# Expert rows gathered in fp32 from the residual rows, one-hot columns that carry the norm factor, separate sums, and weight tiles up to 19 ahead

## The chip, the cores and the metric

The kernel runs on one core of a Trainium2 chip. The metric is the device time of one execution in microseconds (us). TensorE (PE in the profile) multiplies; VectorE (DVE), ScalarE (ACT) and GpSimd (POOL) work elementwise; every DMA is issued from SyncE's queue (SP), in program order.

## The reference

One transformer block over 512 tokens of width 1024, in fp32: a mixer (differential attention and a state-space branch, merged and projected into the residual) and then a mixture of experts. The second part is what the change touches:

```python
x = x + merged @ w_out[l]
h2 = rms_norm(x, norm_ffn_w[l], NORM_EPS)          # x * rsqrt(mean(x*x)+eps) * w
# hierarchical_moe(h2): 64 experts, each token goes to the best 2 of its best group of 8
xb = t[buf_tok].reshape(n_blocks, MOE_BLOCK, d)    # rows of h2, gathered by expert
hid = jax.nn.silu(xblk @ w_gate[e]) * (xblk @ w_up[e])   # 1024 -> 512
yb = hid @ w_down[e]                                      # 512 -> 1024
out = zeros.at[buf_tok].add(yb * buf_w[:, None])
return rms_norm(x + out, final_norm_w, NORM_EPS)
```

All 64 experts' weights are read once: 64 x 6 MB.

## The kernel before

The 512 tokens are four chunks of 128 rows. Up to the output projection the program is ordered by a small planner (`Flow`): each piece of work is a job with an engine, a cost, a priority and the jobs that it waits for, and the jobs are written into the program in the order in which the planner would start them. The last units, `WO0` and `WO1`, are the output projection; their handler `ev_wo` adds the result to the residual rows `x1`, sums squares, transposes the rows, computes the router's logits, and makes the norm factor of each row, `fst[:, 3]`.

*The normed rows.* `ev_wo` also makes h2: VectorE multiplies the residual by the norm's weight (`b`, L1291), ScalarE multiplies by the row's factor and rounds to fp32r (`hh`, the high part `h2H`), and VectorE or GpSimd subtracts to get the low part `h2L` (`hl` L1353, `hd` L1348). These are four big buffers.

*The router.* `route` works on chunks 0 and 1, then on 2 and 3, almost wholly on VectorE: the best group, the two best experts, then the place of each token within its expert (`rank` on TensorE, `rk`). `onehot` (L1434) writes a one-hot matrix `P` for the experts of the next two groups: 128 tokens by 256 slots for each chunk.

*The gather.* `gather_mm` (L1445, L1446) gathers the rows of a 128-column block `k` for 256 slots with eight fp32r matmuls (high and low part of each chunk), and ScalarE copies the result to `xt`.

*The experts.* 19 groups: the first 12 experts in pairs (64 slots each), the others in fours (32 slots each). The order of groups is two pairs, six fours, four pairs, seven fours. For a group, `gate_up` (L1714) multiplies 8 blocks `k` against the gate and up weights, 2 or 4 experts side by side in TensorE's columns; then come the activation, `hidden_t` (transposes), `down` (L1737) and `weighted`. The results go back to the tokens with `combine` (L1753, L1754, and the add to `x1`, L1759), which runs one group later, right after the next group's `gate_up`. After an odd group's `combine` and `hidden_t`, and ahead of its `down`, stands the gather for the next two groups. For the first two groups the gather is spread over group 0's `gate_up` (one block ahead of each `k`).

*The weights.* An expert's weights come as six tiles of 1 MB, each for two blocks `k`: four for gate/up, two for down. `tiles` lists them in the order of use. `issue` sends the next one into a big buffer, into the extra buffer `ewx` or into the pair of staging buffers; `free` and `fill` are called after every second `k`: as many tiles as were used up are counted free, and as many are issued. There are 19 big buffers (`NB`). Two hold `x1`, four `h2H` and `h2L`; so 13 big ones, `ewx` and the staging pair hold weights: 15 tiles. `NS = 4` experts are first in order whatever the counts; the others are placed by counts that group 0 works out (`perm`).

Of the kernel before, what the change touches and what calls it, by code (L numbers as in the profile page):

```python
# [118 lines left out]
def block_kernel(ctx: ExitStack, tc: tile.TileContext, I, out):  # L119
# [1092 lines left out]
    NX = 2  # L1212
    NE = NB - 6 + NX
# [11 lines left out]

    def issue():
        n = nxt["i"]
        nxt["i"] += 1
        kind, e, q = tiles[n]
        if n % NE == XS:  # L1230
            t = [stage(), stage()]
        else:
            b = (mt("ewx", [128, 2048], "ew") if n % NE == 0 else big("ew")).rearrange("p (k n) -> p k n", k=2)
# [5 lines left out]
        if n % NE == XS:  # L1239
# [6 lines left out]
    x1t, h2H, h2L = [], [], []  # L1246
# [4 lines left out]
    def consts():  # L1251
        m = mt("xt", [128, 2048], "rc")
        rc["nfw"] = m[:, :1024]
        nc.sync.dma_start(rc["nfw"], bcast(I["nfw"], D))
        rc["wr"] = m[:, 1024:1600].rearrange("p (k n) -> p k n", k=8)
        nc.sync.dma_start(rc["wr"], I["wr"])
        nft = m[:, 1600:1608]
        nc.sync.dma_start(nft, I["nft"])
        V.tensor_tensor(rc["wr"], rc["wr"], nft.unsqueeze(2).to_broadcast([128, 8, 72]), op=OP.mult)
        rc["lgh"] = m[:, 1608:1896].rearrange("p (c n) -> p c n", c=NCH)  # L1260
        rc["br"] = m[:, 1896:1968]
# [8 lines left out]

    cj = J("Q", 2.5, consts, [fpj, wsl], prio=-1)
# [3 lines left out]
    lgj, lmj, hlj, h2j = {}, {}, {}, {}  # L1275

    def ev_wo(n):
        def f(c, ps, j):
# [7 lines left out]

            def b(i):
                if i == 0:
                    t["hc"] = mt("y" if c else "P", [128, D], "hc")
                o = slice(i * 512, i * 512 + 512)  # L1290
                V.tensor_tensor(t["hc"][:, o], x1(c)[:, o], rc["nfw"][:, o], op=OP.mult)  # L1291
# [50 lines left out]
            def hs():  # L1342
                A.activation(t["hc"], t["hc"], AF.Copy, scale=fst[:, 3, c:c + 1])

            def hd():
                if c % 2 == 0:
                    h2L.append(big("h2L", F32R).rearrange("p (c n) -> p c n", c=2))
                G.tensor_tensor(h2L[c // 2][:, c % 2], t["hc"], h2H[c // 2][:, c % 2].bitcast(F32), op=OP.subtract)  # L1348

            def hl():  # L1350
                if c % 2 == 0:
                    h2L.append(big("h2L", F32R).rearrange("p (c n) -> p c n", c=2))
                V.scalar_tensor_tensor(h2L[c // 2][:, c % 2], t["hc"], fst[:, 3, c:c + 1],  # L1353
                                       h2H[c // 2][:, c % 2].bitcast(F32), op0=OP.mult, op1=OP.subtract)

# [8 lines left out]
            if n == 0:  # L1364
                t["a0"] = a_
            else:
                b_ = J("V", 0.61, lambda: b(0), [t["a0"], cj, hlj[1] if c == 3 else None, j if c < 3 else None],
                       prio=0.7 if c < 2 else 0.12)
                b_ = J("V", 0.61, lambda: b(1), [a_, b_], prio=0.7 if c < 2 else 0.12)
# [14 lines left out]
            else:  # L1384
# [5 lines left out]
                big_ = ["big"] if c % 2 == 0 else []  # L1390
                h_ = J("A", 1.0, hh, [s, b_, h2j.get(c - 1)], prio=2, acq=big_)
                h2j[c] = h_
                pl = hlj.get(c - 1) if c % 2 else None
                if c > 1:
                    h_ = J("A", 1.0, hs, [h_], prio=1)
                    hlj[c] = J("G", 2.35, hd, [h_, pl], prio=0, acq=big_)
                else:
                    hlj[c] = J("V", 1.2, hl, [h_, pl], prio=2, acq=big_)
# [29 lines left out]
    def onehot(es, cs=range(NCH)):  # L1428
        n, w = len(es), E if es[0] < NW else E // 2
        if 0 in cs:  # L1430
            R["P", es[0]] = mt("P", [128, NCH, 256], "P", F32R)
# [7 lines left out]
    def h2(t, c):  # L1439
        return t[c // 2][:, c % 2]  # L1440
# [9 lines left out]
    def route(cl, prev):  # L1450
# [51 lines left out]
        def gat(k):  # L1502
            if cl[0] == 0:
                gb[k] = side()
            gather_mm(R["P0"], 256, gb[k][:, :256], k, cl)
# [17 lines left out]
        kj = J("V", 0.2 + 0.35 * n, rk, [rj, r.get("rk", hlj[0])], prio=pr)  # L1523
        r["rk"] = kj
        last = cl[-1] == NCH - 1
        for k0 in (0, 1):
            j = J("P", 0.22 * n, lambda k0=k0: gat(k0), [kj, lmj[3]] + [hlj[c] for c in cl] + [r.get(("g", k0))],
# [13 lines left out]
    def evac(k):  # L1541
        if k == 0:
            xt[0] = mt("xt", [128, 8, 256], "xt")
        A.activation(xt[0][:, k], gb[k][:, :256], AF.Copy)
# [4 lines left out]
    def weights1():  # L1549
        V.tensor_copy(R["cnt"], R["rps"][:, 256:256 + E])  # L1550
        V.tensor_reduce(R["gs"], R["ge"], axis=AX.X, op=OP.add)
        V.reciprocal(R["gate"], R["gs"])
# [20 lines left out]
    live = {"n": NB - len(fl.tok["big"]) + 1}  # L1573

    def free(n=1):
        live["n"] -= n

    def fill():
        while nxt["i"] < len(tiles) and live["n"] < NB + NX:
            live["n"] += 1  # L1580
            issue()
# [93 lines left out]
    def gather1(P, xt, k):  # L1675
        ps = side()
        gather_mm(P, 256, ps[:, :256], k, range(NCH))
        A.activation(xt[:, k], ps[:, :256], AF.Copy)

    def gather(P, w, xt, ks=range(8), ps={}):  # L1680
        for k in ks:
            if k % 2 == 0:
                ps[0] = side()
            gather_mm(P, w, ps[0][:, (k % 2) * w:(k % 2) * w + w], k, range(NCH))
            if k % 2:
                A.activation(xt[:, k - 1:k + 1], ps[0][:, :2 * w].rearrange("p (k n) -> p k n", k=2), AF.Copy)
# [4 lines left out]
    def slots(P, n, w, wcols):  # L1691
        W = n * w
        ps = side()
        for c in range(NCH):
            T.transpose(ps[:W, c * 128:c * 128 + 128], P[:, c].bitcast(F32), ident)
        pt = mt("pt", [128, 512], "pt", F32R)[:W]
        V.tensor_copy(pt, ps[:W])
        ws = side()
        for c in range(NCH):
            T.matmul(ws[:W, :n], lhsT=P[:, c].bitcast(F32), rhs=wcols(c), start=(c == 0), stop=(c == 3))  # L1700
# [5 lines left out]
    def gate_up(xt, n, w, gu, done, pre=lambda q: None):  # L1706
# [24 lines left out]
    def down(ht, n, w, dn, done):  # L1731
# [25 lines left out]
    def combine_add(ps, c, i):  # L1757
        o = x1(c)[:, i * 512:i * 512 + 512]
        V.tensor_tensor(o, o, ps, op=OP.add)  # L1759

    def combine(pt, yh, yl):
        for c in range(NCH):
            for i in range(2):
                combine_add(combine_mm(pt, yh, yl, c, i), c, i)

    def odd(k):
        free(k % 2)
# [8 lines left out]
    ordering = order_tables()  # L1776
    for gi, g_ in enumerate(groups):
# [210 lines left out]
```

## Time and profile before

| | |
|---|---|
| median of 3 runs | 1835.35 us (1835.19 to 1837.14) |
| profiled execution: its own time | 1836.18 us |
| its span, first to last instruction | 1834.4 us |
| TensorE busy | 1621.0 us (88%) |
| VectorE, ScalarE, GpSimd busy | 786.0, 414.9, 321.4 us |
| read from HBM | 471.56 MB |
| granted TensorE clock, mean | 0.95 |

Up to about 850 us the mixer and its projection run. The expert weights are 403 MB of the 471 MB. A busy TensorE is not one at its peak: matmuls that wait one behind the other for weights count as busy too.

### The profile page before, as it was taken

What the parts mean: (1) busy time and instruction counts of PE and PEld (TensorE: products, weight loads), DVE (VectorE), ACT (ScalarE), POOL (GpSimd) and SP (SyncE); (2) the same over time, 40 slices, a digit from 0 to 9 for tenths busy, and PEclk for the clock granted to TensorE, in tenths of its full rate; (3) what the DMA queues carried; (4) which work ended last, traced back from release to release, by engine and by line L of the source; (5) the groups of instructions that cost most, each with busy time, mean ns of one, the idle gap of its engine ahead of it and who ended that gap; (6) DMA issues with size and microseconds to landing.
All of it is one profiled execution on the core that took longest, in us unless ns stands there. A gap on an engine that the chain in (4) does not pass through costs nothing. (4 is left out here: it accounts for less than half of the span.)

```text
span 1834.4 us, 22989 instructions
## 1 busy us (share of the span) xinstructions
PE 1621.0 (88%) x8767; PEld 995.2 (54%) x8767; DVE 786.0 (43%) x1487; ACT 414.9 (23%) x839; POOL 321.4 (18%) x331
## 2 busy tenths in 40 slices
PE   8999999999999999998996877778998777787785
PEld 6878788878787777887451423124444231132232
DVE  7698842487878765436130521021321211111113
ACT  5355530344444432122110100001011000010001
POOL 5244421153526252102000000000000000000001
PEclk8999999999999999999999889889999898898988
DMA  5321123222121222356899999999999999999995
GB/s 160 102 62 49 53 85 99 70 69 81 59 92 58 69 70 92 92 214 275 335 388 420 419 421 421 420 420 420 421 419 420 421 419 421 421 419 420 421 420 225
DMA packets 81616, 475.19 MB, mean 259 GB/s; under 512 B 10208, under 2 KB 10592, under 8 KB 35808
## 3 DMA queue, kind: packets, MB, share of 16 engines
q1 hardware_dynamic: 81504, 473.70, 65.5%
q8 instruction: 70, 1.15, 0.3%
q14 instruction: 42, 0.34, 0.1%
HBM read 471.56 MB, written 2.10 MB: 258 GB/s over the span
## 5 line engine op out<-in xcount | busy, mean ns | idle before, releaser
L1714 PE MATMUL g<-ew,xt 128*32 128x512 f32 (+1 forms) x1896 | 412.9, 691 | 151.8 <-DMA ew<-in_gu_dram 151.5
L243 PE MATMUL g<-hH,w 128*128 128x512 f32 x1024 | 345.6, 401 | 0.0
L1714 PEld LDWEIGHTS g<-ew,xt 128*32 128x32 f32 (+1 forms) x1896 | 96.2, 128 | 437.9 <-DMA ew<-in_gu_dram 273.8
L1719 DVE SCALAR_TENSOR_TENSOR hh<-hh,g 128x512 f32<-128x512 f32 x19 | 13.1, 687 | 504.9 <-ACT hh L1718 504.9
L243 PEld LDWEIGHTS g<-hH,w 128*128 128x128 f32 x1024 | 192.4, 188 | 43.7 <-issue 6.0
L243 PE MATMUL g<-hL,w 128*128 128x512 f32 x512 | 199.9, 390 | 0.0
L1737 PE MATMUL s<-ew,hT 128*32 128x512 f32 (+1 forms) x968 | 172.3, 653 | 23.0 <-DMA ew<-in_dn_dram 22.1
L1889 POOL TENSOR_TENSOR fst<-fst 128x1 f32<-128x1 f32 x4 | 1.2, 300 | 960.8 <-ACT fo L1882 960.7
L203 DVE TENSOR_TENSOR w<-stg,w 128x1024 fp32r<-128x1024 f32 x108 | 140.8, 1312 | 55.4 <-ACT w L200 32.2
L1718 ACT ACTIVATE hh<-g 128x512 f32<-128x512 f32 x19 | 11.3, 597 | 524.6 <-PE g L1714 524.6
L1737 PEld LDWEIGHTS s<-ew,hT 128*32 128x32 f32 (+1 forms) x968 | 46.3, 122 | 129.9 <-issue 77.7
L198 POOL TENSOR_SCALAR w<-stg 128x1024 fp32r<-128x1024 f32 x60 | 69.7, 1162 | 256.5 <-DMA stg<-in_wu_dram 178.8
L243 PEld LDWEIGHTS g<-hL,w 128*128 128x128 f32 x512 | 96.4, 188 | 16.8
L1759 DVE TENSOR_TENSOR x<-x,s 128x512 f32<-128x512 f32 x152 | 92.4, 678 | 23.0 <-PE s L1754 23.0
L1747 DVE SCALAR_TENSOR_TENSOR yl<-s,sl,yh 128x512 fp32r<-128x512 f32 x38 | 28.4, 751 | 163.8 <-ACT yh L1746 162.6
L848 DVE SCALAR_TENSOR_TENSOR xb<-u,cw,xb 128x511 f32<-128x511 f32 (+2 forms) x96 | 81.7, 861 | 23.4 <-ACT xb L844 21.7
L243 PE MATMUL g<-w,hH 128*128 128x512 f32 x256 | 84.5, 411 | 0.0
L1714 PE MATMUL g<-stg,xt 128*32 128x512 f32 (+1 forms) x152 | 81.6, 673 | 1.7 <-DMA stg<-in_gu_dram 1.6
L243 PE MATMUL g<-sH,w 128*128 128x512 f32 x256 | 80.7, 397 | 0.0
L200 ACT ACTIVATE w<-stg 128x1024 fp32r<-128x1024 f32 x60 | 63.2, 1054 | 76.8 <-DMA stg<-in_wu_dram 63.2
L1445 PE MATMUL s<-P,h2H 128*128 128x256 f32 (+1 forms) x320 | 78.5, 287 | 1.4 <-DVE P L1434 1.4
L1446 PE MATMUL s<-P,h2L 128*128 128x256 f32 (+1 forms) x320 | 76.7, 282 | 0.0
(338 smaller groups left out, 2454.2 us busy)
## 6 DMA issues: line engine op xcount, KB each, us to landing
ew<-in_gu_dram SPq DMA_DIRECT2D x237, 1024.0 KB, 18.3
ew<-in_dn_dram SPq DMA_DIRECT2D x118, 1024.0 KB, 18.5
stg<-in_wu_dram SPq DMA_DIRECT2D x120, 512.0 KB, 3.6
stg<-in_gu_dram SPq DMA_DIRECT2D x38, 512.0 KB, 17.7
stg<-in_dn_dram SPq DMA_DIRECT2D x13, 512.0 KB, 18.0
xT<-in_xT_dram SPq DMA_DIRECT2D x4, 512.0 KB, 5.7
x<-in_xn_dram SPq DMA_DIRECT2D x2, 1024.0 KB, 10.0
out_dram<-fo SPq DMA_DIRECT2D x8, 256.0 KB, 2.1
```

The source lines that it names most:

```text
L198: G.tensor_scalar(c["h"], c["st"], 1.0, 0.0, op0=OP.mult, op1=OP.add)
L200: A.activation(c["h"], c["st"], AF.Copy)
L203: (G if i % 10 == 9 else V).tensor_tensor(c["lo"], c["st"], c["h"].bitcast(F32), op=OP.subtract)
L243: T.matmul(cell[b], lhsT=x, rhs=y, start=first and i == 0, stop=last and i == 2)
L848: V.scalar_tensor_tensor(x()[:, 3 - k:], t["u"][:, :n], w[:, k:k + 1], x()[:, 3 - k:], op0=OP.mult, op1=OP.add)
L1445: T.matmul(o, lhsT=h2(h2H, c)[:, d], rhs=P[:, c], start=(c == 0), stop=False)
L1446: T.matmul(o, lhsT=h2(h2L, c)[:, d], rhs=P[:, c], start=False, stop=(c == NCH - 1))
L1714: T.matmul(o[es_], lhsT=xt[:, k, es_], rhs=gu(e, k)[:, i * 512:i * 512 + 512], start=(k == 0), stop=(k == 7), tile_position=(0, w * e))
L1719: V.scalar_tensor_tensor(hh, hh, 1.0, pg[:W], op0=OP.add, op1=OP.mult)
L1737: T.matmul(ps[i][es_], lhsT=ht[:, k, es_], rhs=dn(e, k)[:, i * 512:i * 512 + 512], start=(k == 0), stop=(k == 3), tile_position=(0, w * e))
L1747: V.scalar_tensor_tensor(yl[:, i], ps[i][:W], sl[:, :1], yh[:, i].bitcast(F32), op0=OP.mult, op1=OP.subtract)
L1759: V.tensor_tensor(o, o, ps, op=OP.add)
```

## The change

The split copies go. The gather multiplies the residual rows `x1` themselves, in fp32, one matmul for each chunk; the one-hot entry is the row's norm factor in place of 1, and the norm's weight is the scale of ScalarE's copy to `xt`. `x1` must therefore stay as it is, and the sums go to two buffers of their own, `acct`: the first `combine` reads `x1` and writes `acct`, the later ones add there. The token weights are divided by the norm factor again (the product with `fst[:, 3]` in `weights1`), and the one-hot for the way back is made by a comparison with 0.

Group 0's interleaved gather fetches only its own 128 slots; those of group 1 are gathered on their own, two blocks ahead of group 0's `down` and six in group 1's `gate_up`. The one-hot for groups 2 and 3 moves from group 0 to the end of group 1's `gate_up`. `issue` takes any free place (`room`): 17 big buffers, `ewx` and the staging pair, 19 tiles; when group 1 begins, two big ones are set aside for `acct`.

```diff
+    homes = []
+    room = {"ewx": 1, "stg": 0, "big": 0}
...
+            home = next(r for r in ("ewx", "stg", "big") if room[r] > (1 if r == "stg" and n < XS else 0))
+        room[home] -= 1
+        homes.append(home)
...
-            def hh():
-                if c % 2 == 0:
-                    h2H.append(big("h2H", F32R).rearrange("p (c n) -> p c n", c=2))
-                A.activation(h2H[c // 2][:, c % 2], t["hc"], AF.Copy, scale=fst[:, 3, c:c + 1])
...
-                G.tensor_tensor(h2L[c // 2][:, c % 2], t["hc"], h2H[c // 2][:, c % 2].bitcast(F32), op=OP.subtract)
...
         for c in cs:
-            V.tensor_tensor(P[:, c].rearrange("p (e s) -> p e s", e=n),
-                            rk1[:, c, es[0]:es[0] + n].unsqueeze(2).to_broadcast([128, n, w]),
-                            iota1[:, None, :w].to_broadcast([128, n, w]), op=OP.is_equal)
+            if es[0] == 0:
+                for e in range(n):
+                    V.tensor_scalar(P[:, c, e * w:e * w + w], iota1[:, :w], rk1[:, c, e:e + 1], fst[:, 3, c:c + 1],
+                                    op0=OP.is_equal, op1=OP.mult)
...
+        if es[0]:
+            scaled(P)
...
-    def gather_mm(P, w, o, k, cs):
+    def scaled(P):
+        V.tensor_tensor(P, P, fst[:, 3].unsqueeze(2).to_broadcast([128, NCH, P.shape[2]]), op=OP.mult)
+
+    def gather_mm(P, o, k, cs):
         d = slice(k * 128, k * 128 + 128)
         for c in cs:
-            T.matmul(o, lhsT=h2(h2H, c)[:, d], rhs=P[:, c], start=(c == 0), stop=False)
-            T.matmul(o, lhsT=h2(h2L, c)[:, d], rhs=P[:, c], start=False, stop=(c == NCH - 1))
+            T.matmul(o, lhsT=x1(c)[:, d], rhs=P[:, c], start=(c == 0), stop=(c == NCH - 1))
+
+    def gathered(xt, k, ps):
+        A.activation(xt[:, k], ps, AF.Copy, scale=rc["nft"][:, k:k + 1])
...
-    live = {"n": NB - len(fl.tok["big"]) + 1}
+    room.update(stg=1, big=len(fl.tok["big"]))
...
         def pre(k):
-            if gi == 0:
-                if 1 <= k < 7:
-                    gather1(P, xt, k + 1)
-                if k in ordering:
-                    ordering[k]()
+            if gi < 2 and 1 <= k < 7:
+                half = slice(128 * gi, 128 * gi + 128)
+                gather(P[:, :, half], xt[:, :, half], [k + 1])
+            if gi == 0 and k in ordering:
+                ordering[k]()
+            if gi == 1 and k == 7:
+                nP[0] = onehot(sum(groups[2:4], []))
...
+        if gi == 1:
+            room["big"] -= 2
...
-            if gi + 2 < NG:
-                es = sum(groups[gi + 2:gi + 4], [])
-                P = onehot(es)
+            if gi == 0:
+                gather(P[:, :, 128:], xt[:, :, 128:], [0, 1])
+            elif gi + 2 < NG:
+                nP[0] = onehot(sum(groups[gi + 2:gi + 4], []))
         elif not last:
-            m = P.shape[2]
-            xt = rows(m)
-            gather(P, m, xt)
+            P = nP[0]
+            xt = rows(P.shape[2])
+            gather(P, xt)
             ps_ = group_slots(P, gi + 1)
```

TensorE between group 0's transposes and group 1's gate/up, before (a row is one matmul, x16 sixteen of them; `hh` and `hT` are the hidden rows, `ident` the identity for transposes):

```order
L1726 MATMUL s<-ident,hh 128x128 x4
L1695 MATMUL s<-ident,P 128x128 x4
L1700 MATMUL s<-ptab,P 128x2 x4
L1737 MATMUL s<-ew,hT 64x512 x16
L1714 MATMUL g<-ew,xt 64x512 x32
```

and now, in the changed program:

```order
L1700 MATMUL s<-ident,hh 128x128 x4
L1669 MATMUL s<-ident,P 128x128 x4
L1674 MATMUL s<-ptab,P 128x2 x4
L1422 MATMUL s<-P,x_6945 128x128 x2
L1422 MATMUL s<-P,x_7000 128x128 x2
L1422 MATMUL s<-P,x_6945 128x128 x2
L1422 MATMUL s<-P,x_7000 128x128 x2
L1711 MATMUL s<-ew,hT 64x512 x16
L1688 MATMUL g<-ew,xt 64x512 x4
L1422 MATMUL s<-P,x_6945 128x128 x2
L1422 MATMUL s<-P,x_7000 128x128 x2
L1688 MATMUL g<-ew,xt 64x512 x4
```

Gather matmuls (L1422) now stand ahead of group 0's down stage, and four of them between the gate/up matmuls of two blocks; this goes on for six blocks of group 1.

VectorE in the router, from the second half's logits of chunk 2 to the first one-hot matrices, before (`x_7000` are the residual rows of chunks 2 and 3, `ht` transposed rows, `lg` logits, `ab` the chosen experts, `ptab` the places):

```order
L1285 SCALAR_TENSOR_TENSOR x_7000<-g,x_7000 128x256 x2
L1327 SCALAR_TENSOR_TENSOR lg<-s,fst,rc 128x72
L1291 TENSOR_TENSOR hc<-x_7000,rc 128x512
L1309 COPY ht<-s 128x256
L1331 TENSOR_TENSOR fst<-fst 128x1
L1332 TENSOR_SCALAR fst<-fst 128x1
L1309 COPY ht<-s 128x256
L1479 TENSOR_TENSOR d_6972<-o_6973,o_6974 128x16
L1480 TENSOR_TENSOR ab<-og,d_6972 128x128
```

and now:

```order
L1459 TENSOR_TENSOR ab<-og,d_6972 128x128
L1295 SCALAR_TENSOR_TENSOR x_7000<-g,x_7000 128x256 x2
L1477 SCALAR_TENSOR_TENSOR ptab<-s,ab 128x128
L1406 TENSOR_SCALAR P<-iota_93,ptab,fst 128x64 x8
L1313 COPY ht<-s 128x256
L1335 TENSOR_TENSOR fst<-fst 128x1
L1336 TENSOR_SCALAR fst<-fst 128x1
L1331 SCALAR_TENSOR_TENSOR lg<-s,fst,rc 128x72
L1313 COPY ht<-s 128x256
```

The router's first half (`ab` of chunks 0 and 1) now stands ahead of the last residual add instead of behind the copies of the transposed rows, and the eight one-hot instructions of chunks 0 and 1 stand ahead of those copies.

## Rows read from the trace of the kernel before

**Rows 1.** Windows: stretch, its length, engines' busy us (instructions), clock, DMA share, GB/s.

```profile
865.00:870.00 5.00, 5.00 (x24) 3.40 (x24) 3.18 (x18) 0.86 (x3) 0.00 (x0) 0.71 0.00 0
...
880.00:890.00 10.00, 10.00 (x59) 5.25 (x60) 0.34 (x2) 1.75 (x5) 0.00 (x0) 1.00 0.82 313
...
930.00:935.00 5.00, 5.00 (x26) 1.72 (x24) 0.00 (x0) 0.00 (x0) 0.00 (x0) 1.00 0.37 107
935.00:940.00 5.00, 5.00 (x43) 1.34 (x42) 1.50 (x2) 1.37 (x2) 0.00 (x0) 1.00 1.01 416
...
1300.00:1400.00 100.00, 98.23 (x522) 50.32 (x520) 29.11 (x56) 12.49 (x20) 0.00 (x0) 1.00 1.02 420
```

**Rows 2.** Waits: SyncE's queue in 860 to 936 us; TensorE in 936 to 1815 us.

```profile
SPq L1243 <- PE s L1737: 23.3, 3, 16.0
...
PE g L1714 <- DMA ew<-in_gu_dram: 151.5, 109, 2.7
```

**Rows 3.** Timeline of SyncE's queue, 915 to 940 us: start, length, engine, instruction.

```profile
915.83 17.38 SPq L1243 DMA_DIRECT2D ew<-in_gu_dram  x3
```

**Rows 4.** Timeline of TensorE's matmuls in groups 0 and 1.

```profile
867.90 1.94 PE L1714 MATMUL g<-ew,xt 128*64 128x512 f32 x8
869.77 0.39 PE L1445 MATMUL s<-P,h2H 128*128 128x256 f32 x1
...
870.91 1.94 PE L1714 MATMUL g<-ew,xt 128*64 128x512 f32 x8
...
901.91 13.90 PE L1714 MATMUL g<-ew,xt 128*64 128x512 f32 x64
915.74 0.50 PE L1753 MATMUL s<-yh,pt 128*128 128x512 f32 x1
...
919.61 0.66 PE L1726 MATMUL s<-ident,hh 128*128 128x128 f32 x4
920.21 0.38 PE L1445 MATMUL s<-P,h2H 128*128 128x256 f32 x1
...
927.88 0.60 PE L1695 MATMUL s<-ident,P 128*128 128x128 f32 x4
...
929.20 0.64 PE L1737 MATMUL s<-ew,hT 128*64 128x512 f32 x1
```

**Rows 5.** Timeline of TensorE: other fp32 matmuls of 128 columns.

```profile
853.53 1.25 PE L303 MATMUL s<-ident 128*128 128x128 f32 x8
...
888.80 1.16 PE L1633 MATMUL s<-ox,tT 128*128 128x128 f32 x8
889.89 0.64 PE L1714 MATMUL g<-stg,xt 128*64 128x512 f32 x1
```

**Rows 6.** Timeline of the router's stretch: TensorE, GpSimd and VectorE.

```profile
847.07 3.02 PE L243 MATMUL g<-w,gt 128*128 128x512 f32 x12
849.13 2.36 POOL L1348 TENSOR_TENSOR h2L<-hc,h2H 128x1024 fp32r<-128x1024 f32 x1 [3.07 <-ACT hc L1343]
849.19 2.33 DVE L1475 SCALAR_TENSOR_TENSOR es<-o,es 128x16 f32<-128x16 f32 x1
...
852.46 0.75 DVE L1285 SCALAR_TENSOR_TENSOR x<-g,x 128x256 f32<-128x256 f32 x2
853.32 0.68 DVE L1291 TENSOR_TENSOR hc<-x,rc 128x512 f32<-128x512 f32 x1
...
857.65 2.34 POOL L1348 TENSOR_TENSOR h2L<-hc,h2H 128x1024 fp32r<-128x1024 f32 x1 [2.44 <-ACT hc L1343]
857.99 2.63 DVE L1434 TENSOR_TENSOR P<-ptab,iota 128x256 fp32r<-128x256 f32 x2
...
862.30 0.18 DVE L1475 SCALAR_TENSOR_TENSOR es<-o,es 128x16 f32<-128x16 f32 x1
...
864.87 0.76 DVE L1434 TENSOR_TENSOR P<-ptab,iota 128x256 fp32r<-128x256 f32 x2
...
871.47 0.53 DVE L1613 TENSOR_SCALAR ox<-iota,ox 64x64 f32<-64x64 f32 x2
```

More of the change, by code (lines that the diff above doesn't have):

```diff
@@ L1269, in x1, with res @@
         return x1t[c // 2][:, c % 2]
+    def res(c):
+        return acct[c // 2][:, c % 2]
     cj = J("Q", 2.5, consts, [fpj, wsl], prio=-1)
@@ L1572, in block_kernel @@
     fl.run()
-    live = {"n": NB - len(fl.tok["big"]) + 1}
+    room.update(stg=1, big=len(fl.tok["big"]))
     def free(n=1):
-        live["n"] -= n
+        for _ in range(n):
+            room[homes.pop(0)] += 1
     def fill():
-        while nxt["i"] < len(tiles) and live["n"] < NB + NX:
-            live["n"] += 1
+        while nxt["i"] < len(tiles) and max(room.values()) > 0:
             issue()
@@ L1672, in overflow_tables, with gather @@
         V.tensor_copy(R["ovi"], ef)
[L1675 to L1680, printed above, removed]
-        for k in ks:
[L1682 to L1686, printed above, removed]
+    def gather(P, xt, ks=range(8)):
+        w = P.shape[2]
+        for k in ks:
+            ps = side()[:, :w]
+            gather_mm(P, ps, k, range(NCH))
+            gathered(xt, k, ps)
     def rows(w):
@@ L1694, in slots @@
         for c in range(NCH):
-            T.transpose(ps[:W, c * 128:c * 128 + 128], P[:, c].bitcast(F32), ident)
+            T.transpose(ps[:W, c * 128:c * 128 + 128], P[:, c], ident)
         pt = mt("pt", [128, 512], "pt", F32R)[:W]
-        V.tensor_copy(pt, ps[:W])
+        V.tensor_scalar(pt, ps[:W], 0.0, None, op0=OP.is_gt)
         ws = side()
         for c in range(NCH):
-            T.matmul(ws[:W, :n], lhsT=P[:, c].bitcast(F32), rhs=wcols(c), start=(c == 0), stop=(c == 3))
+            T.matmul(ws[:W, :n], lhsT=P[:, c], rhs=wcols(c), start=(c == 0), stop=(c == 3))
         sl = pools["mp"].tile([128, 1], F32, name="sl", bufs=2)[:W]
@@ L1729, in hidden_t, with down @@
         return ht
-    def down(ht, n, w, dn, done):
+    def down(ht, n, w, dn, done=lambda k: None):
         ps = [side(), side()]
@@ L1755, in combine_mm, with combine_add, combine @@
         return ps
[L1757 to L1761, printed above, removed]
+    def combine_add(ps, c, i, src=res):
+        h = slice(i * 512, i * 512 + 512)
+        V.tensor_tensor(res(c)[:, h], src(c)[:, h], ps, op=OP.add)
+    def combine(pt, yh, yl, src=res):
         for c in range(NCH):
+            if src is x1 and c % 2 == 0:
+                acct.append(big("acc").rearrange("p (c n) -> p c n", c=2))
             for i in range(2):
-                combine_add(combine_mm(pt, yh, yl, c, i), c, i)
-    def odd(k):
-        free(k % 2)
+                combine_add(combine_mm(pt, yh, yl, c, i), c, i, src)
     def group_slots(P, gi):
@@ L1807, in block_kernel @@
         elif not last:
-            combine(*pend)
+            combine(*pend, src=x1 if gi == 1 else res)
         if last:
@@ L1862, in block_kernel @@
         yo = [yo[:, 0], yo[:, 1]]
-        combine(pt1, *weighted(down(ht, 1, E, lambda e, k: ow["dn", k], odd), E, sl1, yo))
+        combine(pt1, *weighted(down(ht, 1, E, lambda e, k: ow["dn", k]), E, sl1, yo))
     fl.t = {e: 0.0 for e in "PVAGQ"}
@@ L1881, in sqr @@
             def sqr(i=i, c=c, o=o, half=half):
-                A.activation(o[:, half], x1(c)[:, half], AF.Square, accum_out=fst[:, i, c:c + 1])
+                A.activation(o[:, half], res(c)[:, half], AF.Square, accum_out=fst[:, i, c:c + 1])
             j = J("P", 0.43, mm, prio=c, acq=["s"])
@@ L1899, in f1 @@
         def f1(c=c, o=o):
-            A.activation(o[:, 512:], x1(c)[:, 512:], AF.Copy, scale=fst[:, 3, c:c + 1])
+            A.activation(o[:, 512:], res(c)[:, 512:], AF.Copy, scale=fst[:, 3, c:c + 1])
         def f2(c=c, o=o):
```

89 lines of the change are left out of this document (31 added, 58 removed).

## The prediction

> **What bounds the kernel now.** I read the windows first. From about 935 us to the end the weight stream runs at 416 to 420 GB/s without a dip, even in 1300 to 1400 us where TensorE is busy for 98.23 of 100 us; before 935 us it does dip: 0 GB/s at 865 to 870 us, 313 GB/s at 880 to 890 us, 107 GB/s at 930 to 935 us [rows 1]. Then the waits: after 936 us TensorE's large wait is for expert weights (151.5 us in 109 waits), while before 936 us the DMA queue waits for TensorE, once for 16.0 us at a down matmul [rows 2]. So there are two regimes. In the first two expert groups TensorE is the bound and the stream stops for want of buffers; from 935 us on the stream is the bound, and TensorE's idle time pays for what is added to it. The end of the kernel is therefore the moment at which the stream starts for the last time, plus the bytes still to come, plus a tail that the change leaves alone.
>
> That moment can be seen. The queue issues two tiles at 915.83 us and the third of that row only at the row's end, about 932.9 us [rows 3]. Counted in the code, it is tile 35 (from 0): 15 buffers for weights (13 of 19 big ones, the extra one, the staging pair), and 20 tiles given back by then: eight gate/up and four down tiles of group 0, eight gate/up tiles of group 1. Tile 35 needs the first down tiles of group 1, and that down stage starts at 929.20 us, after combine, transposes and the whole gather for groups 2 and 3 [rows 4].
>
> **The change part by part.** After it, two accumulators take the place of the four split copies, so 17 buffers hold weights once group 1 has begun (19 before). By the same count, the tile that waits for the first down tiles of group 1 is number 37. A tile is 1024 KB, at 420 GB/s 2.50 us, so two more tiles sent before the stop are worth -5.0 us. That is all that the extra buffers give: however early the first 19 tiles land, the stream has run dry again before that down stage. What TensorE does between the last work of the router and that down stage then counts in full.
>
> (a) *fp32 gather matmuls of 128 columns.* The trace of before has no gather in fp32, so its price comes from other fp32 matmuls; each stands there as two records. Four with different weights and 128 columns take 888.80 to 889.89 us: 0.136 us a record; the warm-keeping ones take 1.25/8 = 0.156 [rows 5]. Half of the 512-column price below would be 0.217, a quarter 0.109: that is the lower bound, 0.156 the upper, and I take 0.137, the row of the same shape. Group 0's six interleaved gathers cost 8 x 0.137 = 1.10 us each, against 1.14 us now (869.77 to 870.91) [rows 4]: nothing. New on the path are the second half's gathers: two before group 0's down, 16 records, +2.2 us (1.7 to 2.5), and six inside group 1's gate/up, 48 records, +6.6 us (5.2 to 7.5).
>
> (b) *The gather for groups 2 and 3.* Now 64 matmuls, 920.21 to 927.88 us = 7.67 us. Then 32 fp32 matmuls, 64 records of 256 columns. Price: 64 records of 512 columns, two experts side by side, take 13.90 us [rows 4], so one alone would be 2 x 0.217 = 0.434, and 256 columns 0.217; the combine matmuls (one pass, 512 columns, new weights each) take (919.61 - 915.74)/16 = 0.242. Twice the 128-column price would be 0.274, the upper bound. I take 0.23: 14.7 us, +7.0 us (+6.2 to +9.9).
>
> By a rule of the Trainium skill ("FP8 and Floating Point Precision", TensorE Precision Notes) a true fp32 product takes four passes. At 2.4 GHz that makes 0.213 us a matmul at 128 columns and 0.427 at 256, an estimate of 6.8 us for (a) and +6.0 us for (b). The 512-column row fits it (0.869 against 0.853 us), the 128-column row is above it (0.272 against 0.213). By the Trainium skill alone the sum below would be +5.3 us; I go by the rows.
>
> (c) *The start of group 0.* VectorE carries this stretch. TensorE's last output-projection matmul ends near 850.1 us, yet its result is read at 852.46, because VectorE sits in one 128x16 instruction for 2.33 us; the same line takes 0.18 us later. It lies beside a GpSimd subtraction for a split copy (849.13 us), which goes: -2.2 us. The multiply at 853.32 us goes: -0.6. The first one-hot pair took 2.63 us beside another such subtraction and becomes eight 64-column instructions; two of that kind take 0.53 us, so 2.1 us: -0.5. The second pair was undisturbed at 0.76 us and becomes 2.1: +1.3 [rows 6]. That makes -2.0. In the new order the first eight stand ahead of the copy of the last transposed rows and hold up the router's last logits, while the router's first half, no longer delayed, can end before the projection does; I put half a us on the second and take -2.5. Bounds: -4.0 (the eight at 0.18 us each make it -3.3, and the first half is won in full besides) and -1.0 (the logits lose half of the first item).
>
> (d) *At no cost:* the scaling of later one-hot matrices and their new place in group 1 (VectorE, behind 3.5 us of gate/up matmuls; without that cover about 3 us), the scale in the evacuation (ScalarE, next to idle), separate sums in place of x1 (the same add). The gathers of all later pairs of groups grow by 7 us as well, behind the wait for weights: 151.5 us in all.
>
> Sum: 2.2 + 6.6 + 7.0 - 2.5 = +13.3 us until the down stage of group 1, less 5.0 us for two tiles: **+8.3 us**, between 1.7 + 5.2 + 6.2 - 4.0 - 5.0 = +4.1 and 2.5 + 7.5 + 9.9 - 1.0 - 5.0 = +13.9. The profiled execution took 1836.18 us for a span of 1834.4, 0.83 us above the median, so the shift is put on the median: 1835.35 + 8.3 = **1843.6 us**.
>
> **Rivals.** *No change (13 in 100).* If an fp32 gather matmul, two records, cost no more than the two matmuls that it replaces (0.12 us a record at any width here), (a) would be 64 x 0.12 = 7.7 and (b) 0: 7.7 - 2.5 - 5.0 = +0.2 us, 1835.6. For it speaks that the present gather runs at 7.67/64 = 0.12 us with 256 columns; against it that fp32 needs 0.434 us for 512 columns, nearly double the 0.242 of one pass. A price halfway lands near the edge of this case.
>
> *Faster (6 in 100).* The start of group 0 comes so early that the two tiles outweigh the gathers: at the cheap prices of the first rival it must come 6.4 us earlier instead of 2.5 for -3.7 us (1831.6), at mine 14.5 us. The place is VectorE's router chain. For it: both 2.3 to 2.6 us instructions lie there. Against it: what remains is some forty short dependent instructions, and TensorE's projection still ends at 850.1 us.
>
> *Slower still (7 in 100).* The four middle pairs of groups stop the stream a second time. TensorE is at 98.23% there with the stream full [rows 1], and gets 4 x 3.5 = 14 us of gather more, 5.6 tiles; its longest stretch without a release (combine 3.9, transposes 0.6, gather 14.7, slots 1.3) lets 8.2 tiles land: 13.8 of 17. If the lag exceeds about 15, each tile costs 2.5 us; with four tiles, 1853.6.
>
> My forecast has 74 in 100. About 0.2% (3.7 us) is what a measurement of this kernel can tell from no change. The forecast's own bounds are 1839.4 to 1849.2, all slower; with the last rival slower has 81, same 13, faster 6. For 8 in 10 the range reaches from 1838.5 to 1848.5.
>
> **What would show it.** Right: the first gate/up matmul near 865.4 us; 64 records of the gather in about 14.7 us; the down stage of group 1 starting near 942.5 us; a stop of the queue there of well over 16 us; 420 GB/s without a dip afterwards, the middle groups included. Wrong: gather records near 0.12 us, a group 0 that starts before 862 us, a dip of the stream in 1300 to 1420 us, or a tile sent past the stop that the count of 37 does not allow.

## The result and the profile after

The changed kernel takes 1846.89 us (median of 4 runs, 1846.09 to 1848.97), the kernel before, on the same chip, 1835.42 us (4 runs, 1835.19 to 1837.14): a ratio of 1.0062, interval 1.0045 to 1.0080. It is slower, as forecast, by 11.5 us where 8.3 were forecast; the time lies inside the range. Measured once more, on the chip of later runs (after_again), it was 8.8 us slower than the 1837.1 us of the kernel before. The profiled execution took 1846.09 us, its span 1844.3.

The windows of the changed kernel (columns as in [rows 1]: stretch, length, busy time of TensorE, its weight loads, VectorE, ScalarE and GpSimd, then clock, DMA share and GB/s) show where the stream of weights now stops:

```profile
865.00:870.00 5.00, 5.00 (x31) 2.49 (x29) 2.19 (x11) 0.74 (x2) 0.00 (x0) 1.00 0.31 82
880.00:890.00 10.00, 9.96 (x67) 6.50 (x65) 3.20 (x8) 2.16 (x4) 0.00 (x0) 1.00 0.88 318
930.00:935.00 5.00, 5.00 (x24) 4.40 (x24) 0.00 (x0) 1.24 (x4) 0.00 (x0) 1.00 0.00 0
935.00:940.00 5.00, 5.00 (x31) 4.25 (x31) 1.19 (x5) 1.21 (x3) 0.00 (x0) 1.00 0.00 0
945.00:950.00 5.00, 5.00 (x44) 1.48 (x44) 1.50 (x2) 1.38 (x2) 0.00 (x0) 1.00 1.00 421
1300.00:1400.00 100.00, 99.82 (x470) 50.05 (x467) 34.97 (x62) 12.10 (x21) 0.00 (x0) 1.00 1.02 420
```

From 930 to 940 us nothing is moved, where 107 and 416 GB/s stood; from 945 us on the stream is as full as before, in the middle groups too, although TensorE is now at 99.82 of 100 us there. The waits (SyncE's queue, whole kernel; TensorE's for gate/up weights) say the same: one stop of 22.2 us instead of 16.0 [rows 2], and a spare time of TensorE in the later groups that has shrunk from 151.5 to 131.8 us.

```profile
SPq L1252 <- PE s L1711: 58.2, 15, 22.2
```

```profile
PE g L1688 <- DMA ew<-in_gu_dram: 131.8, 97, 2.7
```

SyncE's timeline of the changed kernel has tile 0 and the stop; five tiles stand in the second row, tiles 35 and 36 sent at its start and the third, tile 37, only at 943.04 us:

```profile
788.92 0.43 SPq L1252 DMA_DIRECT2D ew<-in_gu_dram  x1
...
919.76 27.04 SPq L1252 DMA_DIRECT2D ew<-in_gu_dram  x5
```

In the kernel before the row of tile 0 reads:

```profile
790.56 0.43 SPq L1243 DMA_DIRECT2D ew<-in_gu_dram  x1
```

This row matters for every comparison below. Tile 0 is sent ahead of anything that the change touches at the router, yet in the profiles of this study it goes out anywhere from 787.38 to 791.95 us. So I compare stages from it, not from the start of the span. (Of the 1.6 us between these two rows some 0.5 is the change itself: the load of the norm's weight, one issue, no longer stands ahead of tile 0.)

TensorE's timeline of groups 0 and 1, to be laid beside [rows 4]:

```profile
862.72 1.94 PE L1688 MATMUL g<-ew,xt 128*64 128x512 f32 x8
864.59 1.16 PE L1422 MATMUL s<-P,x 128*128 128x128 f32 x8
865.68 0.65 PE L1688 MATMUL g<-ew,xt 128*64 128x512 f32 x2
...
889.50 2.03 PE L1422 MATMUL s<-P,x 128*128 128x128 f32 x16
891.47 1.08 PE L1711 MATMUL s<-ew,hT 128*64 128x512 f32 x4
...
898.38 1.89 PE L1688 MATMUL g<-ew,xt 128*64 128x512 f32 x8
...
919.65 0.50 PE L1727 MATMUL s<-yh,pt 128*128 128x512 f32 x1
...
924.12 14.08 PE L1422 MATMUL s<-P,x 128*128 128x256 f32 x64
938.04 0.60 PE L1669 MATMUL s<-ident,P 128*128 128x128 f32 x4
...
939.36 1.08 PE L1711 MATMUL s<-ew,hT 128*64 128x512 f32 x4
```

Group 1's down stage starts at 939.36 - 788.92 = 150.4 us after tile 0, before at 929.20 - 790.56 = 138.6: +11.8 us, of +13.3 forecast.

What no step of the prediction had is the end. These are the last warm-keeping matmuls (on the identity, results unused), ahead of the overflow loop (which does no pass here), and the first matmuls of the final combine, of before:

```profile
1814.82 1.16 PE L303 MATMUL s<-ident 128*128 128x128 f32 x8
1817.73 0.50 PE L1753 MATMUL s<-yh,pt 128*128 128x512 f32 x1 [1.75 <-DVEq L1834]
```

and of the changed kernel:

```profile
1820.34 1.16 PE L303 MATMUL s<-ident 128*128 128x128 f32 x8
1826.81 0.79 PE L1727 MATMUL s<-yh,pt 128*128 128x512 f32 x1 [5.31 <-issue]
1827.40 0.63 PE L1728 MATMUL s<-yl,pt 128*128 128x512 f32 x1
1827.82 0.63 PE L1727 MATMUL s<-yh,pt 128*128 128x512 f32 x1
```

The last number in brackets is TensorE's idle time ahead of the row: 1.75 us before, 5.31 after, and "issue" means that nothing the profile shows held it. The combine matmuls then follow each other every 0.43 us (before: 16 of them start between 1817.73 and 1821.29, 0.24 apart). The granted clock says why the matmuls are slower; windows of the changed kernel, same columns:

```profile
1820.00:1822.00 2.00, 1.50 (x9) 0.97 (x8) 0.75 (x1) 0.69 (x1) 0.00 (x0) 1.00 0.00 0
1822.00:1825.00 3.00, 0.00 (x0) 0.00 (x0) 0.00 (x0) 0.00 (x0) 0.00 (x0) 1.00 0.04 11
1825.00:1832.00 7.00, 5.19 (x13) 4.08 (x14) 3.28 (x5) 2.83 (x8) 0.92 (x3) 0.51 0.01 2
```

TensorE did nothing from 1821.50 to 1826.81 us; its clock was still full until 1825 us and then at half, 1.2 GHz, until 1832 us. From the warm-keeping matmuls to the end of the span it is 1844.3 - 1820.34 = 24.0 us, before 1834.4 - 1814.82 = 19.6: **+4.4 us**. From tile 0 to the warm-keeping matmuls it is 1031.4 us against 1024.3: **+7.2 us**. Both, less the 1.6 us by which tile 0 was earlier, make the 9.9 us between the two spans.

In 1822 to 1825 us only the DMA engines move something. By the DMA view a queue q8 carries 71 packets of kind "instruction" in the whole kernel, 1.16 MB, so 16 KB each; in the last 300 us of the kernel before, 2,586 of TensorE's records lie in ten of its intervals. So I take q8 for TensorE's code, in packets of about 259 instructions by that count. Its rows for 1822 to 1827 us of the changed kernel, and for 1816 to 1818 us of before (queue, kind: packets, MB, share):

```profile
q8 instruction: 2, 0.03, 2.5%
```

```profile
q8 instruction: 1, 0.02, 3.0%
```

In the changed kernel the packet ahead of these came at 1790.8 us; before, at 1806.9. My theory became this: the change lengthens TensorE's code by 123 instructions (four for each fp32 matmul, two for a one-pass one, counted in the code), and so moves the loop's exit jump to a place in its packet from which the target is not loaded yet. The rival: something that the change does, such as the separate sums, makes the end longer.

### The profile page after: what moved, and what is told of

It reads as the page before. It is cut to its first block, busy times and chain, and to the rows that moved or that the text cites. A ratio compares the mean times of both kernels' runs of the same rounds, so it can differ in the third digit from the quotient of the medians.

```text
span 1844.3 us, 23121 instructions
## 1 busy us (share of the span) xinstructions
PE 1655.2 (90%) x8831; PEld 1033.7 (56%) x8831; DVE 788.4 (43%) x1499; ACT 424.8 (23%) x877; POOL 316.9 (17%) x329
## 3 DMA queue, kind: packets, MB, share of 16 engines
q8 instruction: 71, 1.16, 0.3%
## 5 line engine op out<-in xcount | busy, mean ns | idle before, releaser
L1688 PE MATMUL g<-ew,xt 128*32 128x512 f32 (+1 forms) x1920 | 401.1, 691 | 131.8 <-DMA ew<-in_gu_dram 131.8
L1711 PE MATMUL s<-ew,hT 128*32 128x512 f32 (+1 forms) x960 | 166.7, 640 | 20.2 <-DMA ew<-in_dn_dram 19.5
L1422 PE MATMUL s<-P,x 128*128 128x256 f32 (+1 forms) x704 | 138.8, 355 | 0.0
L1422 PEld LDWEIGHTS s<-P,x 128*128 128x128 f32 x704 | 120.0, 192 | 24.2 <-issue 9.7
L1733 DVE TENSOR_TENSOR acc<-acc,s 128x512 f32<-128x512 f32 x144 | 88.0, 679 | 26.6 <-PE s L1728 26.6
L848 DVE SCALAR_TENSOR_TENSOR xb<-u,cw,xb 128x511 f32<-128x511 f32 (+2 forms) x96 | 81.7, 861 | 23.4 <-ACT xb L844 21.7
L1720 ACT ACTIVATE yh<-s,sl 128x512 fp32r<-128x512 f32 x38 | 26.1, 687 | 188.6 <-PE s L1711 187.5
```

The costliest lines, as they stand in the source:

```text
L848: V.scalar_tensor_tensor(x()[:, 3 - k:], t["u"][:, :n], w[:, k:k + 1], x()[:, 3 - k:], op0=OP.mult, op1=OP.add)
L1422: T.matmul(o, lhsT=x1(c)[:, d], rhs=P[:, c], start=(c == 0), stop=(c == NCH - 1))
L1688: T.matmul(o[es_], lhsT=xt[:, k, es_], rhs=gu(e, k)[:, i * 512:i * 512 + 512], start=(k == 0), stop=(k == 7), tile_position=(0, w * e))
L1711: T.matmul(ps[i][es_], lhsT=ht[:, k, es_], rhs=dn(e, k)[:, i * 512:i * 512 + 512], start=(k == 0), stop=(k == 3), tile_position=(0, w * e))
L1720: A.activation(yh[:, i], ps[i][:W], AF.Copy, scale=sl[:, :1])
L1733: V.tensor_tensor(res(c)[:, h], src(c)[:, h], ps, op=OP.add)
```

## The experiments

Each kernel ran beside the kernel before, whose median was 1837.16 us beside after_warm32, before_warm31, after_15_places and after_gather_behind, 1837.07 beside after_again, after_hold2, after_half_gather and after_split, and 1837.25 beside the other four. "Idle" is TensorE's idle time at the loop's exit, "stages" the time from tile 0 to the last warm-keeping matmuls, "end" from there to the end of the span.

| kernel | median us | ratio to before (interval) | stages | idle | end |
|---|---|---|---|---|---|
| before (profile of the result) | 1835.42 | | 1024.3 | 1.75 | 19.6 |
| changed (profile of the result) | 1846.89 | 1.0062 (1.0045-1.0080) | 1031.4 | 5.31 | 24.0 |
| after_again | 1845.86 | 1.0049 (1.0036-1.0063) | 1031.5 | 5.28 | 24.0 |
| after_warm32 | 1842.59 | 1.0030 (1.0020-1.0039) | 1033.6 | 1.75 | 18.9 |
| before_warm31 | 1840.83 | 1.0019 (1.0010-1.0028) | 1025.7 | 5.03 | 24.0 |
| after_warm14 | 1842.20 | 1.0032 (1.0021-1.0043) | 1031.5 | 1.76 | 19.0 |
| after_warm7 | 1843.13 | 1.0038 (1.0024-1.0051) | 1031.3 | 1.99 | 19.2 |
| after_15_places | 1846.26 | 1.0045 (1.0032-1.0059) | 1032.8 | 4.85 | 23.4 |
| after_hold2 | 1851.47 | 1.0079 (1.0065-1.0093) | 1036.6 | 4.75 | 23.3 |
| after_half_gather | 1840.29 | 1.0018 (1.0009-1.0027) | 1024.8 | 4.77 | 23.1 |
| after_gather_behind | 1842.72 | 1.0029 (1.0016-1.0041) | 1030.0 | 5.00 | 23.7 |
| after_pool_beside | 1848.43 | 1.0061 (1.0049-1.0074) | 1032.9 | 5.01 | 23.7 |
| after_split | 1834.08 | 0.9986 (0.9977-0.9995) | 1022.4 | 1.75 | 19.0 |
| before_split | 1836.20 | 0.9992 (0.9983-1.0001) | 1022.9 | 1.76 | 19.6 |

The profiled execution of after_warm32 was 3.3 us above its median, with a slower start of groups 0 and 1 that its edit doesn't reach; its stages are to be read with that. The same holds for after_gather_behind: its profiled execution was 2.3 us above its median, and 2.0 us of its stages were lost in group 0, ahead of its edit.

**The end: four kernels that differ in length alone.** The edit, in the loop over groups, of after_warm32 (before_warm31 puts one matmul less into the kernel before; after_warm14 and after_warm7 put two and one into each of groups 11 to 17 of the changed kernel):

```diff
         if last:
             keep_warm(8)
+        elif 10 < gi < 17:
+            keep_warm(5)
+        elif gi == 17:
+            keep_warm(2)
```

> The changed kernel with 32 more warm-keeping fp32 matmuls on the identity, five in each of groups 11 to 16 and two in group 17, where TensorE waits for weights; the output is the same. Theory (code fetch at the loop's exit): the +3.6 us between the last warm-keeping matmul and the first of the final combine, and the half clock behind it, come from where TensorE's code lies against the 16 KB packets in which it is loaded; 128 instructions more put the exit of the overflow loop back where the kernel before has it, so the gap falls from 5.3 to about 1.8 us and the time by 4 to 5 us, to about 1842.5 us. Rival (the change's own work, such as the separate sums or the order at the end, makes the end longer): gap and time stay, 1846.9 us, or up to 8.6 us more if the added matmuls stand on the path.

> The kernel before with 31 more warm-keeping matmuls in groups 11 to 17, nothing of the change in it; 124 instructions put the loop's exit where the changed kernel has it. Theory (code fetch): a gap of about 5.3 us and half clock at the end of a kernel that computes just what it did, 1835.4 + 4 to 5 = about 1839.8 us. Rival (the change's own work): 1835.4 us, gap 1.75 us.

Both came out as the theory had them. Here is after_warm32, then before_warm31:

```profile
1825.17 1.16 PE L303 MATMUL s<-ident 128*128 128x128 f32 x8
1828.08 0.50 PE L1727 MATMUL s<-yh,pt 128*128 128x512 f32 x1 [1.75 <-DVEq L1816]
```

```profile
1814.88 1.16 PE L303 MATMUL s<-ident 128*128 128x128 f32 x8
1821.07 0.80 PE L1753 MATMUL s<-yh,pt 128*128 128x512 f32 x1 [5.03 <-issue]
```

The kernel before, with none of the change in it, gets the long end (24.0 us) and is 3.7 us slower; the changed kernel loses it (18.9 us). The rival falls: nothing that the change computes lengthens the end.

> The changed kernel with 14 more warm-keeping matmuls (two in each of groups 11 to 17), 56 instructions. Theory (code packets of 256 instructions; a jump into the next packet is covered, one two packets on isn't): counted from the order, the jump moves from instruction 212 of its packet to 12 of the next one, its target stays in the packet behind that, so it is a jump into the next packet: gap 1.75 us, -4 to -6 us against the changed kernel (about 8.9 us above the kernel before on the same chip as measured by after_again), about +4 us. Rival (any lengthening helps in proportion, or only the full 128 do): gap near 5 us or in between.

> The same with 7 more (one in each of groups 11 to 17), 28 instructions: the jump moves from 212 to 240 in its packet, its target stays two packets on. Theory (packets): gap about 5 us, time as the changed kernel, about 9 us above the kernel before. Rival (any lengthening helps, or a chance of each build): gap well below 5 us.

The first held: idle 1.76 us. The second missed, and came out as its rival had said: 7 matmuls are enough, idle 1.99 us. The medians are 3.7 and 2.7 us below that of after_again, with intervals that touch its own, so I go by the idle time and the end. The DMA view of after_warm7 for 1817 to 1820 us, while the last down matmuls ran, has a packet shortly ahead of the jump, as none of the kernels with a long end has:

```profile
q8 instruction: 1, 0.02, 2.5%
```

So a packet's edge lies between instructions 212 and 240 of my count, not at 256 where I had put it. This reading was made after the miss, but it holds in all fourteen profiles: where the load of the last packet ahead of the loop's exit began 2 to 10 us before the exit's branch (six kernels), idle is 1.75 to 1.99 us; where it began 30 to 31 us before that branch (the eight others), idle is 4.75 to 5.31 us. The count of matmuls doesn't order them: 7, 14 and 32 do the same, and the 31 of before_warm31 make a kernel slower, against the rival that any lengthening helps.

The trace also has the branches themselves. TensorE's sequencer (PEldq) executes three on the loop's line. Here they are for before and for the changed kernel (shortest, median and longest in ns, then first and last start in us):

```profile
L1834 PEldq COMPARE_BRANCH  x3: 101/187/327, 1814.9 to 1817.5; - x3
```

```profile
L1812 PEldq COMPARE_BRANCH  x3: 97/193/3894, 1820.4 to 1826.6; - x3
```

The longest is the middle one, the jump past the loop. It takes 0.33 to 0.64 us in the six kernels and 3.3 to 3.9 us in the eight, where the load of the next packet begins 0.9 to 1.4 us after the branch does. From its end to the first combine matmul all fourteen take 1.15 to 1.24 us. So all of the added idle time lies in the jump, and none in the code behind it.

**The two places.** First I lowered the planner's count alone:

```diff
         if gi == 1:
-            room["big"] -= 2
+            room["big"] -= 4
```

> The changed kernel with the two additional places for weights taken back from group 1 on: 15 hold weights, as before. Theory (the stream's last restart sets the end): tile 35 instead of 37 waits for the first down tiles of group 1, which start at the same time (939.4 us), so two tiles of 2.49 us more are still to come: +5.0 us, 1851.9 us. Rival (the middle pairs of groups or the bytes after them set the end, and the places bought nothing): 1846.9 us.

The time did not move, but the run doesn't decide: its row of SyncE's queue shows six tiles from 921.34 us, and two of them, 35 and 36, went out at 922 us into buffers that were free, without waiting for group 1's down stage. Nothing had been taken away. So the buffers themselves were taken:

```diff
         if gi == 1:
-            room["big"] -= 2
+            room["big"] -= 4
+            held = [big("hold") for _ in range(2)]
+            for h_ in held:
+                V.memset(h_[:, :1], 0.0)
...
+    V.tensor_tensor(held[0][:, :1], held[0][:, :1], held[1][:, :1], op=OP.add)
     keep_warm(4)
```

> The changed kernel itself once more, on the chip of the runs beside it, since the start of a run moved the stages by up to 3 us between profiles. Theory (about 5.5 us of restart and 4.4 us at the loop's exit): 9 to 11 us above the kernel before on the same chip, with 5.3 us between the last warm-keeping matmul and the final combine. Rival (the first measurement was high by chance, and only the end differs): 4 to 5 us above.

> The changed kernel with two big buffers really taken away from group 1 on (allocated, one column set, read before the loop). Run after_15_places lowered only the planner's count: its queue still sent tiles 35 and 36 at about 922 us, into buffers that were free, so nothing was taken away there. Theory (the restart sets the end): tile 35 is the one that stops, two tiles more are still to come when the stream restarts: +5.0 us against after_again. Rival (the places buy nothing): no difference.

The first run is the changed kernel again, the reference for the runs beside it: 8.8 us above before. after_hold2 is 5.6 us above that, and its stages 5.1 us longer: two tiles are worth what the prediction said. Tile 35, third in this row, went out at 944.7 us:

```profile
921.40 27.62 SPq L1252 DMA_DIRECT2D ew<-in_gu_dram  x6
```

**TensorE's work until the stream restarts.** Two chunks of the gather for groups 2 and 3 are left out (with 16 warm-keeping matmuls later, for the length):

```diff
+            if half:
+                for c in (0, 3):
+                    T.matmul(ps, lhsT=x1(c)[:, k * 128:k * 128 + 128], rhs=P[:, c], start=(c == 0), stop=(c == 3))
```

> The changed kernel with two of four chunks left out of the gather for groups 2 and 3 (so their rows are incomplete: half of that sum is not computed), and 16 more warm-keeping matmuls in groups 11 to 17, so that TensorE's code keeps its length. 32 records of 0.2175 us less: group 1's down stage and group 2's first gate/up both start 7.0 us earlier. Theory (TensorE's work until the weights are released sets the end): tile 37 and tile 41 are both sent 7 us earlier, -7 us against after_again. Rival (where the gather stands and not how long it takes, or a later stage, sets the end): less than 2 us.

```profile
925.87 7.17 PE L1662 MATMUL s<-P,x 128*128 128x256 f32 x32
...
934.20 7.09 PE L1716 MATMUL s<-ew,hT 128*64 128x512 f32 x32
```

The gather takes 7.0 us (925.87 to 932.88 us) in place of 13.9, the stages are 6.8 us shorter, the median is 5.6 us lower: at this place TensorE's time is paid nearly one for one.

Then the same gather was moved, whole, behind group 1's down stage:

```diff
-            gather(P, xt)
-            ps_ = group_slots(P, gi + 1)
+            if gi > 1:
+                gather(P, xt)
+                ps_ = group_slots(P, gi + 1)
         yps = down(ht, n, w, wk("dn"), done)
         pend = (pt, *weighted(yps, 128, sl))
+        if gi == 1:
+            gather(P, xt)
+            ps_ = group_slots(P, gi + 1)
```

> The changed kernel with the gather and the slots for groups 2 and 3 behind group 1's down stage instead of ahead of it; the same matmuls in another order, group 2 starts when it did. Theory (the restart sets the end): down starts at about 924 us instead of 939.4, tiles 37 to 40 are sent from 927.8 us and land by about 940 instead of 958, the next ones wait for group 2's first gate/up tiles (about 948.3 us) and land from 953 instead of 958: about -5 us, 1841.9 us. Rival (TensorE's sum of work until group 2, the same in both, or a later stage sets the end): 1846.9 us.

Its TensorE timeline (matmuls; the second row is the gather, the third group 2's gate/up):

```profile
927.73 7.09 PE L1711 MATMUL s<-ew,hT 128*64 128x512 f32 x32 [0.69 <-ACT hT L1702]
934.75 14.08 PE L1422 MATMUL s<-P,x 128*128 128x256 f32 x64
...
949.99 0.62 PE L1688 MATMUL g<-ew,xt 128*32 128x512 f32 x1
```

Tile 37 went out at 931.4 us, 11.5 us earlier than in after_again, but where 5 us less were expected, the median is only 3.1 us lower, with an interval that touches that of after_again (the stages are 1.5 us shorter, 3.5 without the 2.0 us lost in group 0). Four tiles land early, then the stream stops again: tile 41 needs group 2's first gate/up tiles, and that stage starts no earlier. So theory and rival were both half right. The restart matters, but behind it stands TensorE's work until the next release.

The last edit of this series therefore shortens that work as well:

```diff
-            if gi < 2 and 1 <= k < 7:
-                half = slice(128 * gi, 128 * gi + 128)
+            if gi < 3 and 1 <= k < 7:
+                half = slice(128 * (gi > 0), 128 * (gi > 0) + 128)
                 gather(P[:, :, half], xt[:, :, half], [k + 1])
...
-            if gi == 0:
+            if gi in (0, 2):
                 gather(P[:, :, 128:], xt[:, :, 128:], [0, 1])
-            elif gi + 2 < NG:
+            if gi and gi + 2 < NG:
...
+        if gi == 1:
+            gather(P[:, :, :128], xt[:, :, :128])
+            ps_ = group_slots(P, 2)
```

> The changed kernel with the gather for groups 2 and 3 in two halves of 128 columns: group 2's behind group 1's down stage, group 3's inside group 2's gate/up stage, as groups 0 and 1 have it. 64 fp32 matmuls of 128 columns in place of 32 of 256, 128 instructions more, which puts the loop's exit where after_warm32 had it. Theory (after_gather_behind showed that the next stop, tile 41 at group 2's first gate/up tiles, comes next): that stage starts 13.9 - 8.7 = 5.2 us earlier, the stream restarts about 6 to 7 us earlier than in after_again, and the end is 4.5 us shorter: -11 us against after_again, about as the kernel before. Rival (the halves' extra 3.5 us of TensorE time are paid for later): -4.5 us, the end alone.

```profile
924.90 7.09 PE L1711 MATMUL s<-ew,hT 128*64 128x512 f32 x32 [0.69 <-ACT hT L1702]
931.92 7.41 PE L1422 MATMUL s<-P,x 128*128 128x128 f32 x64
939.17 0.60 PE L1669 MATMUL s<-ident,P 128*128 128x128 f32 x4
...
940.49 0.62 PE L1688 MATMUL g<-ew,xt 128*32 128x512 f32 x1
```

The median is 11.8 us below after_again, 11 expected; the profiled executions differ by 13.8 us (stages 9.1, end 5.0, less 0.3 by which tile 0 was later; that of after_split was 2.0 us below its median). At 0.9986 (0.9977 to 0.9995) it beats both kernels, by 3.0 us the one before. The half gather took 7.25 us, less than the 8.7 I had put in.

> The kernel before with the reordering of after_split alone (gather of group 2 behind group 1's down stage, of group 3 inside group 2's gate/up; split copies in fp32r, one shared sum), and 32 warm-keeping matmuls in groups 11 to 17, so that with the 128 instructions of the halves TensorE's code is 256 longer and the loop's exit lies as before. Theory (the restart sets the end here too): group 1's down starts at about 920.2 us instead of 929.2 and tile 35 goes out at about 924 instead of 932.9; group 2's gate/up starts 0 to 3.7 us earlier, by what 64 one-pass matmuls of 128 columns take (3.9 to 7.7 us): -2 to -5 us against the kernel before, about 1833.5. Rival (the kernel before has nothing to gain, since it sends the next stop's tiles no earlier): no difference.

There is no difference that can be measured; the rival holds. Tile 35 was sent at 926.4 us in place of 932.9, 7.9 us earlier when counted from tile 0, but it landed only 2.4 us earlier (936.7 against 937.7 us): the tile ahead of it was still landing, until 934.2 us. Then the queue stopped again, two tiles into the next row:

```profile
929.85 13.61 SPq L1243 DMA_DIRECT2D ew<-in_gu_dram  x3
```

Its third tile went out at 943.1 us, in the kernel before at 939.9, so 1.9 us later from tile 0. What the earlier restart won was lost at this second stop.

Whether the change made the gain of after_split possible is not shown. With the same order of gathers and the short end the two kernels differ little: stages of 1022.4 (after_split) and 1022.9 us (before_split), medians 2.1 us apart, intervals that overlap.

**The start of group 0.** GpSimd gets two subtractions back:

```diff
+            def busy():
+                G.tensor_tensor(mt("y", [128, D], "hc"), x1(c), x1(c), op=OP.subtract)
...
                 lmj[c] = j
+                if c > 1:
+                    J("G", 2.35, busy, [s], prio=0)
```

> The changed kernel with the GpSimd work of the two removed split copies put back for the second half of the rows (two subtractions 128x1024 into a tile that nobody reads, issued as soon as the row statistics are there); no other engine's order changes. Theory (a VectorE instruction that lies beside such a subtraction takes as long as it): one or two short router instructions take about 2.3 us instead of 0.2 to 0.4; the first may fall in VectorE's wait for the projection, the second lies on the way from the last logits to the one-hot matrix: group 0's gate/up starts 2.2 to 4.5 us later, the time is 2 to 4 us above the changed kernel's. Rival (VectorE's long instruction had another cause): group 0 starts near 862.6 to 863.9 us as in the other profiles of the changed kernel, and the time stays.

GpSimd's rows, then two of VectorE's:

```profile
847.95 1.90 POOL L1342 TENSOR_TENSOR hc<-x 128x1024 f32<-128x1024 f32 x1
...
854.44 1.89 POOL L1342 TENSOR_TENSOR hc<-x 128x1024 f32<-128x1024 f32 x1
```

```profile
848.29 1.58 DVE L1453 TENSOR_TENSOR o<-d,gx 128x16 f32<-128x16 f32 x1
...
854.51 1.91 DVE L1327 SCALAR_TENSOR_TENSOR rc<-rc,fst 128x72 f32<-128x72 f32 x1
```

In the changed kernel these two take 0.18 and 0.29 us. Beside a subtraction they end when it ends (849.87 and 849.85 us, 856.42 and 856.33). That shows the mechanism of the prediction's 2.2 us. By the Trainium skill ("SBUF — State Buffer", Terms) VectorE and GpSimd arbitrate for one port pair, and the loser is blocked for a whole instruction; these rows agree. The size was missed: group 0 starts 75.3 us after tile 0 instead of 73.8, +1.5 us and not 2.2 to 4.5, because the first long instruction falls in VectorE's wait for the projection, 1.15 us in the changed kernel. In the time (1.0061 against 1.0049, intervals that overlap) it can't be told.

## Why the prediction was right, and where it was not

The forecast was slower, by a restart of the weight stream that comes later; after_half_gather and after_hold2 show that this is what bounds the time. Step by step, from tile 0:

- **(a)** The two gathers ahead of group 0's down stage: 889.50 to 891.47 us, +2.0 (forecast 2.2). The six inside group 1's gate/up: that stage takes 898.38 to 919.65 us, 21.3 against 13.8 [rows 4], +7.4 (6.6). One costs 1.09 us (864.59 to 865.68), as taken from [rows 5]. The 0.9 us beyond 6 x 1.09 are a term that the sum left out: a row of eight gate/up matmuls takes 1.87 us between gathers (862.72 to 864.59) and 1.74 in the unbroken row of 64 (13.90/8) [rows 4].
- **(b)** 924.12 to 938.04 us = 13.9 us, 0.2175 a record: +6.2, the lower bound, half of the 512-column price, and not the 0.23 that I chose. The four passes of the Trainium skill ("FP8 and Floating Point Precision", TensorE Precision Notes) fit here: an estimate of 0.427 us a matmul, measured 0.435.
- **(c)** Group 0 starts 862.72 - 788.92 = 73.8 us after tile 0, before 867.90 - 790.56 = 77.3: -3.5 (forecast -2.5). This is the term that was mis-sized most. The eight first one-hot instructions do hold up the last logits a little. But in the new order they no longer stand between these logits and the second half's one-hots, where the undivided pair had taken 2.63 us [rows 6]; I had taken off only 0.5 for it.
- **Sum** +12.1 by these rows, +11.8 measured until group 1's down stage, 13.3 forecast. **Two tiles** -5.0; after_hold2 measured 5.6 on the median, 5.1 in the stages. Tile 37 was the one that stopped, as counted. The stages came out at +7.2, forecast +8.3.
- **The step that failed**, though the time lies in the range, is the clause "plus a tail that the change leaves alone". The end is 4.4 us longer, 3.6 of idle time at the loop's exit and the rest at the half clock behind it. The experiments put that down to where TensorE's code stands against the packets in which it is loaded: the jump past the loop took 3.89 us in place of 0.33.

The rivals: *no change* needed gather records near 0.12 us, those of the large gather take 0.2175. *Faster* needed a start 6.4 us earlier, it came 3.5 us earlier; *slower still* needed a dip of the stream in the middle groups, which stayed at 420 GB/s. Group 0's first gate/up matmul came at 862.72 us where 865.4 were forecast, near the 862 us that were named as a sign of being wrong; 1.6 us of that are tile 0's, 1.0 are (c)'s. That the median came within 3.3 us of the forecast owes something to luck: in my sum the stages were 1.1 us too long and the end 4.4 us too short, and with 28 instructions more (after_warm7) the same end would have been 4.8 us shorter. The difference between the two measurements of the change, 11.5 and 8.8 us, is within what their intervals allow.

By the Trainium skill ("Runtime: NRT & Kernel Launch", Instruction fetch mechanics) code comes in blocks of 256 instructions, the next one is fetched while the current one runs, and a taken branch out of that window waits for its target. The trace agrees with the size (16 KB a packet) and with the stall, here 3.0 to 3.6 us more idle time. That all of it lies in the branch agrees as well.

## What to carry to other kernels

Ask of each stage what it releases, and count TensorE's work up to that release and to the next one: moving a gather behind one release gave 3.1 us of the 5 expected, because the next release came no earlier. A branch near the end is part of the sum: whenever a change alters an engine's instruction count, look at the idle time behind the jump and at the instruction queue's packets, and if the jump has become expensive, lengthen the code where the engine waits anyway. Compare stages from an event ahead of the change, since executions differ by some us before it.

## What was not expected of the hardware

- A loop that does no pass cost 3.7 us more (before_warm31) for 31 matmuls added in groups 11 to 17, where TensorE had time.
- In the 5.3 us without work TensorE's granted clock fell to half, 1.2 GHz, and stood there for about 7 us in the changed kernel; across the 1.75 us of the kernel before it stayed at full.
- An fp32 matmul of 128 columns costs 0.113 us a record in a row of 64 (after_split, 7.25 us), but 0.136 in rows of eight between other matmuls: some 0.18 us more for each such row.
